# The decay of a chunk in a recurrence: applied to the state's sums instead of to `b` and `k`, with small operand steps on ScalarE

## The chip, the cores and the metric

The kernel runs on one core of one Trainium2 chip. The metric is the device time of one execution in microseconds. A run is one execution on the chip; the time of a kernel is the median of its runs.

## What is computed

The reference is two blocks of a network over 256 tokens of width 1024. The first block has two layers; each has a gated feed-forward part, a mixing part with a recurrence (RWKV-7, eight heads of 64) beside a block attention, a cross attention to a memory of 256 tokens, and a second feed-forward part. The second block (chunked mLSTM, differential attention, a mixture of experts) isn't touched. The change lies in the recurrence, which the reference states as a scan over tokens, cut here to its core:

```python
    kk = kk / jnp.maximum(jnp.sqrt(jnp.sum(kk * kk, axis=-1, keepdims=True)), 1e-12)
    b = kk * a

    def step(state, inp):
        r_t, w_t, k_t, v_t, kk_t, b_t = inp
        sa = jnp.einsum('bhij,bhj->bhi', state, -kk_t)
        state = (state * w_t[:, :, None, :] + sa[..., None] * b_t[:, :, None, :]
                 + v_t[..., None] * k_t[:, :, None, :])
        return state, jnp.einsum('bhij,bhj->bhi', state, r_t)
```

## The kernel before

All of it is one program in which each engine works through its own list. The weights of the projections are read from memory as `raw`, split by ScalarE into a high part `wh` and by VectorE into the rest `wl`, and multiplied on TensorE in three products (`wh` with `XH`, `wl` with `XH`, `wh` with `XL`); a unit of weights is 128x1024. These products, shown as `mm` or `acc` with `wh` or `wl`, are most of TensorE's time.

The recurrence is computed in chunks of 64 tokens. Each layer has two groups of four heads (group 0 and 1). For a group, `rwkv_early` builds the operands from the projections: decays as running products (`Pc`, and its inverse `rP`, both tiles `el`), `AR` (the rows of minus `kk` and of `r`, times the decay) and `BK` (`b` and `k`, divided by the decay), for two halves `t` of 128 tokens. `pe` holds `Pc` at the last token of each chunk. A chunk's first column of `AR` has no decay and is written by a step of its own over 128x2 elements. `rwkv_solve` inverts a small triangular matrix `W` for both halves on VectorE, in fourteen steps of a product and a sum (`t1k<-W`, `W<-W,t1k`); the result goes to memory and comes back as `c` (`c<-W`, four transfers on SyncE), and VectorE spreads it into `Y`.

`rwkv_chunk` then does one half: transposes of `Y`, three products that finish the inverse, the solution `ZW` of the chunk's own equations, the scores `gr`, the outputs `YL`, and for each chunk the sums `ST` of the state with, for the middle chunks, a matrix `M` that carries the state on. Before the change `BK` is first multiplied on GpSimd with the decay to the chunk's end (`bkh`, 128x256, two a half), transposed on TensorE and evicted as `bkt`; the sums `ST` are products with `bkt` that ScalarE copies out of PSUM, and `M` adds a diagonal of the decays (`dg`, a tile `t1k` from GpSimd). `rwkv_late` carries the state over the chunks 1 and 2, adds the state's part to `YL`, and normalises it. A reciprocal root of that normalisation is a power on GpSimd.

What stands where is set by a planner while the program is written out. All parts of the mixing stage (both groups, the projections, the block attention `moba` with its tiles `bi` and `sm`, the memory's keys) are generators. Each ends a piece with

```python
        yield 0.86, self.due(y, RH)
```

that is TensorE's cost of the next piece by an estimate, and the time at which what it needs will be there by the planner's own clock, which notes every instruction at L378. The weaver puts weight products in until the piece is due. So a due time that is dropped or moved changes what stands beside it on every engine. Since all instructions pass L378, rows of the profile carry that line, and the tiles' names tell them apart. The mixing stage of the first layer lies at about 200 to 420 us, that of the second at about 896 to 1116 us.

Of the kernel before, what the change touches and what calls it, by code (L numbers as in the profile page):

```python
# [13 lines left out]
AF = mybir.ActivationFunctionType  # L14
OP = mybir.AluOpType
# [4 lines left out]
P = 128  # L20
# [427 lines left out]
class Prog:  # L448
# [525 lines left out]
    def rwkv_early(self, l, g, lo, rT, kT, need):  # L974

        nc = self.nc
        tt, stt, ts = nc.vector.tensor_tensor, nc.vector.scalar_tensor_tensor, nc.vector.tensor_scalar
        mm, tr, act = nc.tensor.matmul, nc.tensor.transpose, nc.scalar.activation
# [8 lines left out]
        sq, d, rd = (self.k("el", 512) for _ in range(3))  # L987
# [4 lines left out]
        s = self.ps("tr")  # L992
# [22 lines left out]
        Pc, rP = self.k("el", 512), self.k("el", 512)  # L1015
# [10 lines left out]
        for b in range(2):  # L1026
            z = self.ps("tr")
# [11 lines left out]
        cut = lambda z, t: z.rearrange("p (b t c s) -> p t b c s", b=2, t=2, c=2)[:, t]  # L1039
        t3 = lambda z, t: z.rearrange("p (b t s) -> p t b s", b=2, t=2)[:, t]  # L1040
        pe = self.k("pe", 8)
        pev = pe.rearrange("p (t b c) -> p t b c", t=2, b=2)
        AR, BK = [], []
        for t in range(2):
            nc.vector.tensor_copy(pev[:, t], cut(Pc, t)[:, :, :, 63])
            ar = self.k("AR", 512).rearrange("p (b k c s) -> p b k c s", b=2, k=2, c=2)
            bk = self.k("BK", 512).rearrange("p (k b s) -> p k b s", k=2, b=2)
            for c in range(2):
                kc, pc = cut(kk, t)[:, :, c], cut(Pc, t)[:, :, c]
                stt(ar[:, :, 0, c, 1:], kc[:, :, 1:], -1.0, pc[:, :, :63], op0=OP.mult, op1=OP.mult)  # L1050
                ts(ar[:, :, 0, c, 0], kc[:, :, 0], -1.0, None, op0=OP.mult)
            arm = ar.rearrange("p b k c s -> p b k (c s)")
            stt(bk[:, 0], t3(bT, t), -0.5, t3(rP, t), op0=OP.mult, op1=OP.mult)
            stt(bk[:, 1], t3(kp, t), -1.0, t3(rP, t), op0=OP.mult, op1=OP.mult)
            tt(arm[:, :, 1], t3(rT, t), t3(Pc, t), op=OP.mult)
            AR.append(arm)
            BK.append(bk)
            yield 0, -0.8
# [4 lines left out]
    def rwkv_late(self, l, g, lo, E, rkp, vT, Y, need, C):  # L1063
# [20 lines left out]
        for cc in (1, 2):  # L1084
            sp = self.ps("acc")
            for b in range(2):
                mm(sp[:, b * 64:(b + 1) * 64], M[cc][:, bs(b)], ST[cc][:, b * 64:(b + 1) * 64], start=True, stop=True)
            tt(ST[cc + 1], sp[:, :128], ST[cc + 1], op=OP.add)
            yield 0.43, self.due(ST[cc + 1])


# [101 lines left out]
    def rwkv_chunk(self, g, t, E, vT, DT, YL, M, ST, W, small, solved):  # L1193
# [85 lines left out]
        tt(rv, rv, rp, op=OP.add)  # L1279
        yield 0.86, self.due(rv)  # L1280
        ZW = solve(1)

        bh = []
        for i in range(2):
            z = self.k("bkh", 256)
            nc.gpsimd.tensor_tensor(z.rearrange("p (h d) -> p h d", d=64), BK[t][:, i].rearrange("p b (c s) -> p (b c) s", c=2),
                                    pev[:, t].rearrange("p b c -> p (b c)")[:, :, None].to_broadcast([P, 4, 64]), op=OP.mult)
            bh.append(z)
        yield 0.86, 0

        gr = self.k("gr", 1024).rearrange("p (b k i s) -> p b k i s", b=2, k=2, i=2)
        for par, gp in enumerate(self.heads2(BK[t], AR[t], 1)):
            tt(gr[:, :, par], gp.rearrange("p (b i s) -> p b i s", b=2, i=2),
               self.cst("mr")[:, None, None, :].to_broadcast([P, 2, 2, P]), op=OP.mult)
        yield 0.95, self.due(*bh)
        tp = self.ps("tr")
        for b in range(2):
            tr(tp[:, bs(b)], bh[0][:, bs(b)], self.ident)
            tr(tp[:, bs(2 + b)], bh[1][:, bs(b)], self.ident)
        bkt = self.k("bkt", 512)  # L1300
        act(bkt, tp, AF.Copy)
        tb, tk = bkt[:, :256], bkt[:, 256:]
# [17 lines left out]
        for c_ in range(2):  # L1320
            cc = 2 * t + c_
            rows = slice(c_ * 64, c_ * 64 + 64)
            if cc in (1, 2):
                mp = self.ps("acc")
                for b in range(2):
                    mm(mp[:, bs(b)], ZW[rows, 1, 2 * b:2 * b + 2].rearrange("p h d -> p (h d)"), tb[rows, bs(b)],
                       start=True, stop=True)
                dg = self.k("t1k", 256)
                nc.gpsimd.tensor_tensor(q2(dg), both(self.ident, 2),
                                        pev[:, t, :, c_:c_ + 1].to_broadcast([P, 2, P]), op=OP.mult)  # L1330
                m = self.k("M", 256)
                tt(q2(m), q2(mp[:, :256]), both(self.cst("bd"), 2), op=OP.mult)
                tt(m, m, dg, op=OP.add)
                M[cc] = m
                yield 0.43, 0
            if cc < 3:
                qp = self.ps("acc")
                for h in range(4):
                    b, par = divmod(h, 2)
                    o = qp[par * 64:par * 64 + 64, b * 64:(b + 1) * 64]  # L1340
                    mm(o, tb[rows, hs(h)], ZW[rows, 0, h], start=True, stop=False)
                    mm(o, tk[rows, hs(h)], tv[rows, hs(h)], start=False, stop=True)
                ST[cc + 1] = self.k("ST", 128)
                act(ST[cc + 1], qp[:, :128], AF.Copy)
                yield 0.7, 0
        yield 0, 0.7

# [1033 lines left out]
    def beyond(self, state, out):  # L2381
# [13 lines left out]
        with self.tc.If(most > P):  # L2395
# [18 lines left out]

BUFS = dict(s16=4, s8=8, ss=2, rs=4, rh=6, s2=4, t1k=4, bi=1, sm=1, pt=1, nr=2,
            omu=1, lora=1, rkv=10, waup=1, gup=1, half=1, kaf=1, sg=1,
            el=5, pe=2, AR=3, BK=3, bkh=2,
            ak=1, tokv=2, bkt=2, RH=2, ZW=2, A=2, Y=2, X=2, T1=2, M=2, ST=3, gr=1, K=2,
            DT=2, YL=2, W=1, c16=2)

# [69 lines left out]
```

## Time and profile before

| | us |
|---|---|
| median of 3 runs | 1950.87 |
| lowest, highest | 1950.57, 1951.28 |
| the profiled run | 1949.61 |
| its span | 1947.6 |

The profile is of one execution. Its span is the time from the first instruction to the last; about 2 us lie around it. A wait is idle time of an engine just before an instruction, with the instruction that ended it (the releaser). The engines are PE (TensorE), DVE (VectorE), ACT (ScalarE), POOL (GpSimd) and SP (SyncE, which issues the transfers); matmul rows of TensorE overlap, so a product of 0.39 us starts about 0.23 us behind the last.

### The profile page before, as it was taken

How to read it: one execution, taken by the hardware profiler on the slowest of the kernel's cores; microseconds unless marked ns; L12 is line 12 of the kernel's file. 1: busy time of each engine (PE TensorE's matmuls, PEld its weight loads, DVE VectorE, ACT ScalarE, POOL GpSimd, SP SyncE). 2: the span in 40 equal slices, each digit the busy share in tenths (PEclk: the TensorE clock that was granted, in tenths of full speed). 3: DMA queues.
4: the chain of work that ended last, by engine and by line, in shares of the span. 5: the costliest groups of instructions: out<-in, count | busy, mean ns of one | idle time of the engine just before them, and what ended most of it. 6: DMA issues, size and time to landing. Idle time of an engine off the chain costs nothing.

```text
span 1947.6 us, 26262 instructions
## 1 busy us (share of the span) xinstructions
PE 1897.4 (97%) x9534; PEld 1532.9 (79%) x9534; DVE 1403.1 (72%) x2287; ACT 1059.3 (54%) x1606; POOL 73.3 (4%) x69
## 2 busy tenths in 40 slices
PE   8999999999999999999999999999999999999997
PEld 6888778888888878888787888888777786877775
DVE  6666787664666676666877655666687677999897
ACT  4444653655544444445536655444555546777674
POOL 0000011000000000000110000000001000000000
PEclk9999999999999999999999999999999999999999
DMA  8766432244566656665314253666564453999996
GB/s 280 249 223 226 128 126 68 86 155 159 172 211 222 216 205 215 220 213 173 134 41 127 97 189 117 222 221 215 183 202 139 150 182 139 337 340 360 332 337 223
DMA packets 114806, 381.41 MB, mean 196 GB/s; under 512 B 17080, under 2 KB 21864, under 8 KB 114544
## 3 DMA queue, kind: packets, MB, share of 16 engines
q1 hardware_dynamic: 114672, 379.68, 58.3%
q8 instruction: 77, 1.26, 0.3%
q14 instruction: 57, 0.47, 0.1%
HBM read 378.03 MB, written 3.17 MB: 196 GB/s over the span
## 4 chain that ended last, share of the span: by engine, by line
PE 76%; issue 11%; DVE 7%; ACT 2%; POOL 1%; DMA 1%; SPq 0%; DVEq 0%; POOLq 0%; ACTq 0%
PE mm L378 40%; PE acc L378 31%; PE tr L378 6%; DVE wl L378 3%; ACT wh L378 1%; POOL rs L378 1%; DVE el L378 1%; DVE s L378 1%; DMA raw<-in_w_dram 1%; DVE XL L378 0%; DVE t1k L378 0%; DVE AR L378 0%; DMA K<-in_mem_dram 0%; DMA x<-in_x_dram 0%; ACT s L378 0%
## 5 line engine op out<-in xcount | busy, mean ns | idle before, releaser
L378 DVE TENSOR_TENSOR wl<-raw,wh 128x1024 fp32r<-128x1024 f32 x648 | 785.2, 1223 | 320.2 <-ACT wh L378 317.2
L378 ACT ACTIVATE wh<-raw 128x1024 fp32r<-128x1024 f32 x648 | 676.3, 1057 | 522.6 <-PE mm L378 295.3
L378 PE MATMUL mm<-wh,XH 128*128 128x512 f32 (+1 forms) x1456 | 579.6, 400 | 3.0 <-ACT s L378 2.4
L378 PE MATMUL mm<-wl,XH 128*128 128x512 f32 (+1 forms) x1456 | 573.5, 394 | 2.6 <-DVE wl L378 2.1
L378 PE MATMUL mm<-wh,XL 128*128 128x512 f32 (+1 forms) x1456 | 571.3, 393 | 0.3
L378 PEld LDWEIGHTS mm<-wl,XH 128*128 128x128 f32 x1456 | 274.4, 188 | 65.7 <-DVE wl L378 10.7
L378 PEld LDWEIGHTS mm<-wh,XH 128*128 128x128 f32 x1456 | 274.7, 189 | 63.5 <-ACT s L378 3.8
L378 PEld LDWEIGHTS mm<-wh,XL 128*128 128x128 f32 x1456 | 274.2, 188 | 57.9 <-DVE XL L378 1.1
L378 PE MATMUL acc<-wh,X 128*128 128x512 f32 x352 | 143.0, 406 | 0.0
L378 PE MATMUL acc<-wh,T 128*128 128x512 f32 x352 | 139.1, 395 | 0.0
L378 PE MATMUL acc<-wl,X 128*128 128x512 f32 x352 | 139.1, 395 | 0.0
L378 PE MATMUL acc<-wl,XH 128*128 128x512 f32 x288 | 115.0, 399 | 2.9 <-DVE wl L378 2.7
L378 PE MATMUL acc<-wh,XH 128*128 128x512 f32 x288 | 114.5, 404 | 0.9 <-ACT XH L378 0.5
L378 PE MATMUL acc<-wh,XL 128*128 128x512 f32 x288 | 114.0, 396 | 0.0
L378 PE MATMUL acc<-wh,ah 128*128 128x512 f32 x256 | 85.7, 396 | 1.3 <-ACT ah L378 1.3
L378 DVE SCALAR_TENSOR_TENSOR el<-raw,vecs,el 128x512 f32<-128x512 f32 x84 | 63.1, 751 | 32.9 <-DMA raw<-in_w_dram 31.1
L378 PEld LDWEIGHTS acc<-wh,T 128*128 128x128 f32 x352 | 66.3, 188 | 15.9
L378 PEld LDWEIGHTS acc<-wl,X 128*128 128x128 f32 x352 | 66.4, 189 | 13.8
L378 PEld LDWEIGHTS acc<-wh,X 128*128 128x128 f32 x352 | 66.3, 188 | 13.4
L378 POOL TENSOR_TENSOR rs<-s,emh 128x2 f32<-128x2 f32 (+2 forms) x28 | 31.6, 1133 | 1147.3 <-DVE s L378 1144.7
L378 PEld LDWEIGHTS acc<-wl,XH 128*128 128x128 f32 x288 | 54.7, 190 | 18.3 <-DVE wl L378 7.5
L378 PEld LDWEIGHTS acc<-wh,XH 128*128 128x128 f32 x288 | 54.4, 190 | 12.5 <-ACT XH L378 1.2
(377 smaller groups left out, 2060.5 us busy)
## 6 DMA issues: line engine op xcount, KB each, us to landing
raw<-in_w_dram SPq DMA_DIRECT2D x696, 512.0 KB
ext<-ext SPq DMA_DIRECT2D x1, 2048.0 KB
K<-in_mem_dram SPq DMA_DIRECT2D x8, 256.0 KB
x<-in_x_dram SPq DMA_DIRECT2D x4, 256.0 KB
bi<-ext SPq DMA_DIRECT2D x4, 256.0 KB
sm<-ext SPq DMA_DIRECT2D x4, 256.0 KB
w<-gates SPq DMA_DIRECT2D x2, 512.0 KB
out_dram<-x SPq DMA_DIRECT2D x4, 256.0 KB
```

What stands on the lines that cost most here:

```text
L378: r = f(*args, **kw)
```

## The change

`BK` is no longer multiplied with the decay before it is transposed, so the eight `bkh` products of a layer and their tile are gone, and the transposes read `BK` itself, without waiting for a due time of `bkh`. The decay is applied to what is summed: the eviction of `ST` from PSUM is made in two halves of 64 columns with the decay of the chunk as a scale per partition, and in `rwkv_late` the addition of the carried state becomes two steps of 64 columns that scale the product and add. `M` then needs a plain identity in place of the diagonal of decays, so the four `t1k` products of GpSimd are gone as well. Two kinds of small steps move from VectorE to ScalarE: the copies `pe`, and the first column of `AR`.

```diff
--- before.py
+++ after.py
@@ -1042,13 +1042,13 @@
         pev = pe.rearrange("p (t b c) -> p t b c", t=2, b=2)
         AR, BK = [], []
         for t in range(2):
-            nc.vector.tensor_copy(pev[:, t], cut(Pc, t)[:, :, :, 63])
+            act(pev[:, t], cut(Pc, t)[:, :, :, 63], AF.Copy)
             ar = self.k("AR", 512).rearrange("p (b k c s) -> p b k c s", b=2, k=2, c=2)
             bk = self.k("BK", 512).rearrange("p (k b s) -> p k b s", k=2, b=2)
             for c in range(2):
                 kc, pc = cut(kk, t)[:, :, c], cut(Pc, t)[:, :, c]
                 stt(ar[:, :, 0, c, 1:], kc[:, :, 1:], -1.0, pc[:, :, :63], op0=OP.mult, op1=OP.mult)
-                ts(ar[:, :, 0, c, 0], kc[:, :, 0], -1.0, None, op0=OP.mult)
+                act(ar[:, :, 0, c, 0], kc[:, :, 0], AF.Copy, scale=-1.0)
             arm = ar.rearrange("p b k c s -> p b k (c s)")
             stt(bk[:, 0], t3(bT, t), -0.5, t3(rP, t), op0=OP.mult, op1=OP.mult)
             stt(bk[:, 1], t3(kp, t), -1.0, t3(rP, t), op0=OP.mult, op1=OP.mult)
@@ -1085,7 +1085,9 @@
             sp = self.ps("acc")
             for b in range(2):
                 mm(sp[:, b * 64:(b + 1) * 64], M[cc][:, bs(b)], ST[cc][:, b * 64:(b + 1) * 64], start=True, stop=True)
-            tt(ST[cc + 1], sp[:, :128], ST[cc + 1], op=OP.add)
+            for b in range(2):
+                sb = slice(b * 64, (b + 1) * 64)
+                stt(ST[cc + 1][:, sb], sp[:, sb], E.out[2][:, cc // 2, b, cc % 2:cc % 2 + 1], ST[cc + 1][:, sb], op0=OP.mult, op1=OP.add)
             yield 0.43, self.due(ST[cc + 1])
 
 
@@ -1279,24 +1281,18 @@
         tt(rv, rv, rp, op=OP.add)
         yield 0.86, self.due(rv)
         ZW = solve(1)
-
-        bh = []
-        for i in range(2):
-            z = self.k("bkh", 256)
-            nc.gpsimd.tensor_tensor(z.rearrange("p (h d) -> p h d", d=64), BK[t][:, i].rearrange("p b (c s) -> p (b c) s", c=2),
-                                    pev[:, t].rearrange("p b c -> p (b c)")[:, :, None].to_broadcast([P, 4, 64]), op=OP.mult)
-            bh.append(z)
         yield 0.86, 0
 
         gr = self.k("gr", 1024).rearrange("p (b k i s) -> p b k i s", b=2, k=2, i=2)
         for par, gp in enumerate(self.heads2(BK[t], AR[t], 1)):
             tt(gr[:, :, par], gp.rearrange("p (b i s) -> p b i s", b=2, i=2),
                self.cst("mr")[:, None, None, :].to_broadcast([P, 2, 2, P]), op=OP.mult)
-        yield 0.95, self.due(*bh)
+        yield 0.95, 0
+
         tp = self.ps("tr")
         for b in range(2):
-            tr(tp[:, bs(b)], bh[0][:, bs(b)], self.ident)
-            tr(tp[:, bs(2 + b)], bh[1][:, bs(b)], self.ident)
+            tr(tp[:, bs(b)], BK[t][:, 0, b], self.ident)
+            tr(tp[:, bs(2 + b)], BK[t][:, 1, b], self.ident)
         bkt = self.k("bkt", 512)
         act(bkt, tp, AF.Copy)
         tb, tk = bkt[:, :256], bkt[:, 256:]
@@ -1325,12 +1321,9 @@
                 for b in range(2):
                     mm(mp[:, bs(b)], ZW[rows, 1, 2 * b:2 * b + 2].rearrange("p h d -> p (h d)"), tb[rows, bs(b)],
                        start=True, stop=True)
-                dg = self.k("t1k", 256)
-                nc.gpsimd.tensor_tensor(q2(dg), both(self.ident, 2),
-                                        pev[:, t, :, c_:c_ + 1].to_broadcast([P, 2, P]), op=OP.mult)
                 m = self.k("M", 256)
                 tt(q2(m), q2(mp[:, :256]), both(self.cst("bd"), 2), op=OP.mult)
-                tt(m, m, dg, op=OP.add)
+                tt(q2(m), q2(m), both(self.ident, 2), op=OP.add)
                 M[cc] = m
                 yield 0.43, 0
             if cc < 3:
@@ -1341,7 +1334,8 @@
                     mm(o, tb[rows, hs(h)], ZW[rows, 0, h], start=True, stop=False)
                     mm(o, tk[rows, hs(h)], tv[rows, hs(h)], start=False, stop=True)
                 ST[cc + 1] = self.k("ST", 128)
-                act(ST[cc + 1], qp[:, :128], AF.Copy)
+                for b in range(2):
+                    act(ST[cc + 1][:, b * 64:(b + 1) * 64], qp[:, b * 64:(b + 1) * 64], AF.Copy, scale=pev[:, t, b, c_:c_ + 1])
                 yield 0.7, 0
         yield 0, 0.7
 
@@ -2414,7 +2408,7 @@
 
 BUFS = dict(s16=4, s8=8, ss=2, rs=4, rh=6, s2=4, t1k=4, bi=1, sm=1, pt=1, nr=2,
             omu=1, lora=1, rkv=10, waup=1, gup=1, half=1, kaf=1, sg=1,
-            el=5, pe=2, AR=3, BK=3, bkh=2,
+            el=5, pe=2, AR=3, BK=3,
             ak=1, tokv=2, bkt=2, RH=2, ZW=2, A=2, Y=2, X=2, T1=2, M=2, ST=3, gr=1, K=2,
             DT=2, YL=2, W=1, c16=2)
```

What each engine then has in its list: TensorE has the same products and transposes; GpSimd has 24 instructions less and VectorE 16 less; ScalarE has 8 `pe`, 16 `AR` and 12 more `ST`. The order differs in these places.

TensorE, first layer, at the start of group 1's chain: transposes of `Y` (`tr<-csts,Y`) and what stands around them. `K` are the memory's keys, `mm` with `wh` or `wl` the weight products. Before:

```order
L378 MATMUL mm_3293<-wh_3165,XL_3190 128x512
L378 MATMUL mm_3293<-wh_3165,XH_3189 128x512
L378 MATMUL mm_3293<-wl_3166,XH_3189 128x512
L378 MATMUL tr_3228<-csts,K_3224 128x128 x4
L378 MATMUL tr_3237<-csts,Y_2793 128x128 x4
L378 MATMUL mm_3293<-wh_3165,XL_3190 128x512
L378 MATMUL mm_3292<-wh_3296,XH_3189 128x512
L378 MATMUL mm_3293<-wh_3296,XH_3189 128x512
L378 MATMUL mm_3292<-wl_3297,XH_3189 128x512
L378 MATMUL tr_3244<-csts,Y_2876 128x128 x4
L378 MATMUL tr_3251<-csts,K_3226 128x128 x4
L378 MATMUL acc_3272<-X_3242,A_2794 128x128 x4
```

The transposes of `Y` stand among weight products and those of `K`. The same engine and place after:

```order
L378 MATMUL mm_3071<-wl_3141,XH_1754 128x512
L378 MATMUL mm_3071<-wh_3140,XL_1755 128x512
L378 MATMUL mm_3071<-wh_3140,XH_1754 128x512
L378 MATMUL mm_3071<-wl_3141,XH_1754 128x512
L378 MATMUL mm_3071<-wh_3140,XL_1755 128x512
L378 MATMUL tr_3169<-csts,Y_2815 128x128 x4
L378 MATMUL tr_3177<-csts,Y_2852 128x128 x4
L378 MATMUL acc_3190<-X_3174,A_2816 128x128 x4
L378 MATMUL acc_3198<-X_3182,A_2853 128x128 x4
L378 MATMUL acc_3206<-Y_2815,T_737_3195 128x128 x4
L378 MATMUL acc_3212<-Y_2852,T_739_3203 128x128 x4
L378 MATMUL acc_3218<-RH_2849,Y_2815 128x128 x4
```

Ahead of both stand weight products; the transposes of `K` are behind the chain now, and the products of the chain follow one another without weight products between.

ScalarE, first layer, group 1: the softmax of the block attention (`bi`, `sm`) with the copies of weights (`wh`) around it. Before:

```order
L378 ACTIVATE sm_3186,s_787_3360<-sm_3186,s_778_3312 128x128 x2
L378 ACTIVATE sm_3186,s_788_3363<-sm_3186,s_779_3315 128x256 x2
L378 ACTIVATE wh_3368<-raw_3294 128x1024
L378 ACTIVATE bi_3183<-bi_3183,s_792_3378 128x128 x2
L378 ACTIVATE bi_3183<-bi_3183,s_793_3382 128x256 x2
L378 ACTIVATE sm_3186<-sm_3186,s_794_3386 128x128 x2
L378 ACTIVATE sm_3186<-sm_3186,s_795_3390 128x256 x2
L378 ACTIVATE ZW_3399<-acc_3394 128x512
L378 ACTIVATE ZW_3406<-acc_3401 128x512
L378 ACTIVATE wh_3416<-raw_3336 128x1024
```

A weight copy stands between the exponentials and the normalisations, and the next behind two evictions. ScalarE at the normalisations after:

```order
L378 ACTIVATE bi_3348<-bi_3348,s_813_3491 128x128
L378 ACTIVATE XH_3362<-s_807_3469 128x4x128
L378 ACTIVATE s_810_3482,ss_3364<-K_3460 128x512
L378 ACTIVATE XH_3362<-s_809_3478 128x4x128
L378 ACTIVATE s_811_3484,ss_3364<-K_3462 128x512
L378 ACTIVATE bi_3348<-bi_3348,s_813_3491 128x128
L378 ACTIVATE bi_3348<-bi_3348,s_814_3495 128x256 x2
L378 ACTIVATE sm_3351<-sm_3351,s_815_3499 128x128 x2
L378 ACTIVATE sm_3351<-sm_3351,s_816_3503 128x256 x2
L378 ACTIVATE wh_3533<-raw_3156 128x1024
L378 ACTIVATE rkv_1981<-acc_3539,vecs 128x256
```

The squares of the keys (`s,ss<-K`) and the whole softmax now stand ahead of the next weight copy `wh_3533`.

VectorE, first layer, group 0, second half of the operands. Before:

```order
L378 SCALAR_TENSOR_TENSOR AR_2173<-el_2101,el_2091 128x2x63
L378 TENSOR_SCALAR AR_2173<-el_2101 128x2
L378 SCALAR_TENSOR_TENSOR AR_2173<-el_2101,el_2091 128x2x63
L378 TENSOR_SCALAR AR_2173<-el_2101 128x2
L378 SCALAR_TENSOR_TENSOR BK_2174<-el_2102,el_2092 128x256
L378 SCALAR_TENSOR_TENSOR BK_2174<-el_2103,el_2092 128x256
L378 TENSOR_TENSOR AR_2173<-rkv_1877,el_2091 128x2x128
L378 SCALAR_TENSOR_TENSOR rkv_1980<-tr_2182,omu_1786,sh_95 128x256
```

Each product of 63 columns is followed by a step of one column per head pair. The same engine and place after:

```order
L378 SCALAR_TENSOR_TENSOR AR_2173<-el_2101,el_2091 128x2x63 x2
L378 SCALAR_TENSOR_TENSOR BK_2174<-el_2102,el_2092 128x256
L378 SCALAR_TENSOR_TENSOR BK_2174<-el_2103,el_2092 128x256
L378 TENSOR_TENSOR AR_2173<-rkv_1877,el_2091 128x2x128
L378 SCALAR_TENSOR_TENSOR rkv_1980<-tr_2182,omu_1786,sh_95 128x256
L378 TENSOR_TENSOR Y_2221<-acc_2223,csts 128x2x128
```

The two steps of one column are gone from between the products; on ScalarE they stand behind an eviction `s<-mm`, and `pe` stands ahead of a weight copy.

## Rows read from the trace of the kernel before

**Rows 1.** the page, busy time by engine, and two groups of the costliest

```profile
PE 1897.4 (97%) x9534; PEld 1532.9 (79%) x9534; DVE 1403.1 (72%) x2287; ACT 1059.3 (54%) x1606; POOL 73.3 (4%) x69
...
L378 DVE TENSOR_TENSOR wl<-raw,wh 128x1024 fp32r<-128x1024 f32 x648 | 785.2, 1223 | 320.2 <-ACT wh L378 317.2
L378 ACT ACTIVATE wh<-raw 128x1024 fp32r<-128x1024 f32 x648 | 676.3, 1057 | 522.6 <-PE mm L378 295.3
```

**Rows 2.** TensorE's waits, 195 to 420 us: waited for: us, times, longest

```profile
PE tr L378 <- DVE el L378: 1.6, 1, 1.6
PE tr L378 <- DVE rkv L378: 1.5, 1, 1.5
...
PE tr L378 <- DVE YL L378: 1.0, 1, 1.0
PE tr L378 <- DMA K<-in_mem_dram: 0.7, 1, 0.7
PE acc L378 <- DVE BK L378: 0.7, 1, 0.7
...
PE mm L378 <- ACT XH L378: 0.2, 1, 0.2
```

**Rows 3.** timeline of TensorE: start, duration, instruction [idle before <-releaser]

```profile
327.47 0.44 PE L378 MATMUL tr<-csts,YL 128*128 128x128 f32 x2 [1.02 <-DVE YL L378]
...
339.62 1.04 PE L378 MATMUL tr<-csts,K 128*128 128x128 f32 x8
...
346.72 0.60 PE L378 MATMUL tr<-csts,Y 128*128 128x128 f32 x4
...
1042.56 0.63 PE L378 MATMUL tr<-csts,K 128*128 128x128 f32 x4 [0.67 <-DMA K<-in_mem_dram]
```

**Rows 4.** timeline of GpSimd, 225 to 345 us

```profile
241.59 3.91 POOL L378 TENSOR_TENSOR bkh<-BK,pe 128x256 f32<-128x256 f32 x2 [6.87 <-DVE BK L378]
...
277.51 1.27 POOL L378 TENSOR_TENSOR t1k<-csts,pe 128x256 f32<-128x256 f32 x2 [5.87 <-DMA c<-W]
```

**Rows 5.** timeline of VectorE, 234 to 250 us

```profile
235.63 0.16 DVE L378 COPY pe<-el 128x4 f32<-128x4 f32 x1
...
244.24 0.59 DVE L378 TENSOR_SCALAR AR<-el 128x2 f32<-128x2 f32 x1
```

**Rows 6.** tile AR: count, ns min/median/max, first and last start, form

```profile
L378 DVE TENSOR_SCALAR AR<-el x16: 156/160/590, 240.8 to 996.8; 128x2 f32<-128x2 f32 x16
...
L378 DVE TENSOR_TENSOR AR<-rkv,el x8: 409/418/840, 235.7 to 996.9; 128x256 f32<-128x256 f32 x8
```

**Rows 7.** tile ST, the same columns

```profile
L378 ACT ACTIVATE ST<-acc x12: 257/278/279, 301.7 to 1082.9; 128x128 f32<-128x128 f32 x12
```

**Rows 8.** timeline of ScalarE, 319 to 400 us

```profile
342.80 0.61 ACT L378 ACTIVATE s<-K 128x512 f32<-128x512 f32 x1
...
354.33 0.40 ACT L378 ACTIVATE bi<-bi,s 128x128 f32<-128x128 f32 x1 [1.45 <-DVE s L378]
...
358.80 1.48 ACT L378 ACTIVATE bi<-bi,s 128x128 f32<-128x128 f32 x4
...
394.87 0.47 ACT L378 ACTIVATE rkv<-acc,vecs 128x256 f32<-128x256 f32 x1 [0.38 <-PE acc L378]
```

**Rows 9.** timeline of VectorE, 319 to 365 us

```profile
327.56 0.22 DVE L378 TENSOR_TENSOR t1k<-W 32x72 f32<-32x72 f32 x1
...
338.44 1.63 DVE L378 TENSOR_TENSOR wl<-raw,wh 128x1024 fp32r<-128x1024 f32 x1
...
340.45 0.20 DVE L378 TENSOR_TENSOR W<-W,t1k 32x28 f32<-32x28 f32 x1
...
344.62 1.27 DVE L378 TENSOR_TENSOR Y<-c,csts 128x512 f32<-128x512 f32 x2
```

**Rows 10.** timeline of SyncE's queue, 323 to 345 us

```profile
340.68 2.68 SPq L378 DMA_DIRECT2D c<-W  x4
```

**Rows 11.** stretches of 10 us: busy by engine, PEclk granted, DMA share, GB/s

```profile
280.00:290.00 10.00, 8.36 (x50) 7.22 (x50) 9.05 (x20) 4.44 (x8) 0.00 (x0) 0.69 0.10 27
```

## The prediction

> **What bounds the kernel now.** First the busy times: TensorE works 97% of the span, no other engine over 72%, GpSimd 4% [rows 1]. So the change, which takes nothing from TensorE's own list, can only pay or cost where TensorE stands idle. Next, the list of its waits in the mixing stage of the first layer: some 8.5 us in eleven places, of which the list shows the larger ones [rows 2]. Two of them, 1.6 us behind `el` and 1.5 us behind `rkv`, and 0.7 us behind `BK`, end on VectorE steps that prepare the recurrence's operands; 1.0 us ends on `YL` (the recurrence's outputs of head group 0); 0.7 us on a transfer of `K` and 0.2 us on `XH`. The second layer shows the same pattern 696 us later: its wait for `K` is 0.67 us, at 1042.56 [rows 3], against the 0.7 us of the list. I therefore work out one layer and take it twice. Outside these two stages TensorE's order hardly moves, and I count nothing there.
>
> **What is taken from VectorE and GpSimd: gains.** Per layer GpSimd loses eight products with the decay (`bkh`) and four small diagonals (`t1k<-csts,pe`); VectorE loses four copies `pe` and eight `AR` columns, which go to ScalarE. What the GpSimd products cost is seen beside them: at 241.59 two `bkh` take 3.91 us [rows 4], and inside that time a VectorE step over two columns takes 0.59 us [rows 5], where such a step has a median of 0.16 us [rows 6]. VectorE's path to `rkv` holds two slow ones, each some 0.50 us from start to start, two fast ones and two `pe` copies, some 0.07 us each from start to start behind a row of 0.16 us [rows 5]: 2 x 0.50 + 4 x 0.07 = 1.3 us. All of it stands before waits of TensorE of 0.7 and 1.5 us [rows 2], so I count it whole: **-1.3 us** (-1.1 to -1.4). ScalarE takes the columns beside this: it has room, and each delays the step behind it by about 0.1 us, which the longer waits behind cover. In group 1 the product `AR<-rkv,el`, 840 ns at its slowest against a median of 418 ns [rows 6], is the one beside GpSimd's diagonals at 277.51 [rows 4]; it loses 0.4 us, the copies another 0.1 us, and a step of about 0.2 us comes in ahead of the scan. It lies before the wait for `el`, 1.6 us [rows 2]: **-0.4 us** (-0.3 to -0.5), allowing 0.1 us for `pe` on ScalarE ahead of an eviction.
>
> **The state's scaling.** An eviction of `ST` on ScalarE, 128x128 in 278 ns at the median [rows 7], becomes two of 128x64 with a scale read from memory. No row shows that form. The lower bound is one row's 0.28 us for both, the upper two rows of a scaled eviction of 128x256, 0.47 us each [rows 8]. I take 0.55 us for the pair, since half the columns lie nearer the lower row. Six such pairs a layer are +1.6 us on ScalarE. VectorE's addition of two states becomes two of half the width, four pairs a layer. Neither lies ahead of a wait of TensorE now; the matmuls on the state have evictions of other tiles around them. I carry the most of this, and three like places (a transpose waits for `bkt`, a product for `A`, `tokv` for `ak`), as small waits: **+0.65 us** (0.3 to 0.8). The Trainium skill (ScalarE: Activation LUTs, What ACT_TABLE_LOAD costs) gives 186 ns plus 0.833 ns a column for an activation, and some 93 ns more for a scale by pointer: 0.49 us for a row of 256 columns, near the 0.47 us of the trace, and 0.57 us for the pair if their overlap of 93 ns holds. The same page of the Trainium skill (Rules for kernel authors) sends plain multiplications to VectorE and speaks against this part; by it the sum would not move by 0.1 us, as long as ScalarE waits for TensorE there.
>
> **What the new order costs.** The planner weaves the recurrence with projections by its own costs, and dropping two due times has moved more than the edit shows. Three places count.
>
> (a) *The end of group 0.* One ScalarE copy of weights now stands ahead of the squares of `YL`, and one VectorE residual ahead of their sums, 1.06 and 1.22 us [rows 1]; before, they stood behind. The wait for `YL` is now 1.0 us [rows 2]. TensorE has 26 products ahead of it in place of 18 in two pieces, so part is covered: **+0.7 us** (0 to 1.4).
>
> (b) *The start of group 1.* Call T the second transpose of `YL`, 327.47 [rows 3]. Before, TensorE does 48 weight products, eight transposes of `s` up to 339.62 (some 12.15 us), then eight of `K`, the scores, 11 more products and four of `K`, and only at 346.72 the transposes of `Y` [rows 3]. That work covers the triangular solve on VectorE. In the new order 42 products and eight transposes stand there. A product is some 0.23 us, since 48 of them and about 1.2 us of transposes are the 12.15 us; less six it is 10.8 us, and the rest has gone behind the chain. The solve itself is not shortened: it runs from 327.56 to 340.65 [rows 9], 13.1 us; without the diagonals on GpSimd [rows 4] the residual beside one of them falls from 1.63 us [rows 9] to the usual 1.22 us [rows 1], less 0.4 us, and a small step of 0.2 us comes in: T + 12.9 us. Then its result goes through memory: four transfers, whose issues alone take 2.68 us [rows 10]. `Y` started 3.97 us after the solve's end [rows 9], but VectorE was busy until then, so that is the upper bound; the lower is the 2.2 us from the end of group 0's solve, 275.34, to 277.51, where GpSimd stopped waiting for these transfers [rows 4]. I take 3.0 us. The first half of `Y` (1.27 us for two [rows 9]) adds 0.65 us. `Y` is there at T + 16.6 us, TensorE at T + 10.8 us: a wait of 5.8 us (5.0 to 6.8), where 0.9 us stood behind `K` and `XH` [rows 2]: **+4.9 us** (4.1 to 5.9). What moved behind the wait can't win it back, since TensorE shows no wait from 346.72 to the end of the stage to fill.
>
> (c) *The chain of group 1 and the softmax.* The chain now runs without weight products in between, so two evictions in a row show: **+0.4 us** (0.2 to 0.6). The attention's softmax comes behind the scores, that is some 20 us later, and with the norms of `K` it stands on ScalarE ahead of the weight copy that TensorE needs 24 products later. Ahead of that copy ScalarE has the eight exponentials (354.33 to 358.80 less a weight copy between them, 3.4 us), four squares of `K` (0.61 us and a read of some 0.2 us each, 3.2 us), four `XH` of the same width (2.4 us) and the normalisations (twice four in 1.48 us) [rows 8], some 12.0 us; ahead of the first lie three VectorE steps of the width of a half of `Y`, 1.9 us [rows 9], between them some evictions of the chain, 0.7 us, and behind them the copy of 1.06 us [rows 1]: 15.7 us. TensorE has about 13 us until then (24 products at 0.23 us are 5.5 us, the rest the end of the chain as it stands in the trace): **+2.7 us** (1.5 to 3.5).
>
> On SyncE the next layer's gate weights and the bias now stand ahead of the weight transfers; two units are loaded ahead, and I cost it at nothing. If that cover is gone, it is up to 1 us.
>
> **Sum.** A layer: -1.3 - 0.4 + 0.65 + 0.7 + 4.9 + 0.4 + 2.7 = +7.65 us; both +15.3 us. The profiled run took 1949.61 us, so 1964.9 us; it was 1.26 us below the median, so 1966.2 us, say 1966. All bounds low: +4.2 us a layer, 1959; all high: +10.8 us, 1972.
>
> **Rivals.** *The new waits are hidden* (0.18). One place decides, TensorE at the transposes of `Y` in group 1. Were `Y` there by T + 10.8 us, because the solve runs further ahead of `YL` than I read, the 0.9 us of old waits would go too, and with no other loss the change leaves -1.3 - 0.4 - 0.9 = -2.6 us a layer: 1945.7. For it: VectorE loses work before the solve, and the 1.0 us behind `YL` shows that the outputs, not the solve, were last. Against: in the new order only the first of the solve's fourteen steps stands wholly ahead of `YL`. *Half of it* (0.14): the wait at `Y` is about 2.5 us, because transfers land at once and the solve's steps close up, and the softmax copy is nearly in time; +4.9 and +2.7 become about +1.6 and +0.8, and the layer is near +1.5 us: within 1947 to 1955. *The clock falls too* (0.14). After the waits at 277 to 283 us the granted clock is 0.69 in 280 to 290, the lower level of 1.2 GHz for a part of it [rows 11]; the longer wait before `Y` could do the same in each layer. A mean of 0.69 is 6.2 of the ten at 1.2 GHz and the rest at 2.4; TensorE was busy 84% of them, so 6.2 x 0.84 / 2 = 2.6 us is the price a layer: 1966.2 + 5.2 = 1971.4. Against: that row follows three waits and a transpose-bound stretch, and one wait between long busy stretches may do less. *The columns on ScalarE delay its evictions* and eat the first gain: 2.6 us more, 1968.8, inside the range.
>
> **How the numbers follow.** The forecast alone has 0.50 (1959 to 1972), the clock 0.14, the half case 0.14, the hidden waits 0.18, anything slower still 0.04. The range of 8 in 10 runs from 1946, which cuts off about half of the hidden case, to 1974. About 0.2% of the time, 3.9 us, is what a measurement can tell: faster 0.18, the same 0.14, slower 0.68.
>
> **What would show it.** In the trace after: no wait of TensorE behind `BK` and `rkv` worth over 1 us in each layer, a wait of 5 to 7 us at the transposes of `Y` about 20 us after the last `ST` of group 0, and one of 1.5 to 3.5 us behind `wh` some 45 us later. The forecast is wrong if the wait at `Y` is under 2 us, or if the moved work meets a wait that I have not seen.

## The result, and the profile after

The changed kernel takes 1967.65 us in the median of 5 runs (1965.17 to 1970.58); the kernel before, on the same chip, 1950.57 us (1948.84 to 1951.28). The ratio is 1.0088, with a 95% interval of 1.0076 to 1.0100: slower by 17.1 us, where the forecast was 1966 us. The profiled execution took 1970.58 us with a span of 1968.7 us, some 3 us more than the median.

The page after, busy time by engine, to set beside [rows 1]:

```profile
PE 1905.0 (97%) x9534; PEld 1537.2 (78%) x9534; DVE 1400.3 (71%) x2271; ACT 1066.8 (54%) x1642; POOL 49.6 (3%) x45
```

VectorE lost 2.8 us and GpSimd a third of its time, ScalarE gained 7.5 us. TensorE has the same 9534 instructions and is busy 7.6 us longer; the span grew by 21.1 us. So this is a story of waits of TensorE and of slower products. Its waits in the first layer's mixing stage, 195 to 440 us (us, times, longest):

```profile
PE tr L378 <- DVE Y L378: 5.6, 2, 5.0
PE mm L378 <- ACT wh L378: 1.9, 1, 1.9
PE tr L378 <- DVE el L378: 1.8, 1, 1.8
...
PE tr L378 <- DVE YL L378: 1.0, 2, 0.7
PE acc L378 <- ACT pt L378: 0.7, 1, 0.7
...
PE tr L378 <- DVE rkv L378: 0.5, 1, 0.5
...
PE acc L378 <- DVE BK L378: 0.3, 1, 0.3
PE acc L378 <- ACT X L378: 0.2, 1, 0.2
```

Beside [rows 2], `rkv` fell from 1.5 to 0.5 us and `BK` from 0.7 to 0.3 us, the waits for `K` and `XH` are gone, and two large ones are new: 5.6 us behind `Y` and 1.9 us behind `wh`, with 0.7 us behind `pt`. The list adds up to 14.6 us. That of before adds up to 8.2 us (not to the 8.5 us of the prediction). The second layer's reads the same within 0.4 us at each of these. The places in TensorE's timeline (start, duration, instruction [idle before <-releaser]):

```profile
283.28 3.30 PE L378 MATMUL acc<-X,A 128*128 128x128 f32 x16 [0.25 <-ACT X L378]
...
328.19 0.44 PE L378 MATMUL tr<-csts,YL 128*128 128x128 f32 x2 [0.30 <-DVE YL L378]
...
344.24 1.09 PE L378 MATMUL tr<-csts,Y 128*128 128x128 f32 x4 [4.96 <-DVE Y L378]
345.93 1.09 PE L378 MATMUL tr<-csts,Y 128*128 128x128 f32 x4 [0.60 <-DVE Y L378]
346.81 2.86 PE L378 MATMUL acc<-X,A 128*128 128x128 f32 x16
...
353.33 2.01 PE L378 MATMUL acc<-ZW,A 128*128 128x128 f32 x16
...
384.50 0.74 PE L378 MATMUL mm<-wh,XH 128*128 128x512 f32 x2 [1.89 <-ACT wh L378]
```

The prediction's T, the second transpose of `YL`, is 328.19 here. TensorE ran out of work at 344.24 - 4.96 = 339.28, that is T + 11.1 us (T + 10.8 us was forecast), and went on at T + 16.05 us (T + 16.6 us was forecast). What held it is on VectorE and in SyncE's queue, the rows that answer to [rows 9] and [rows 10]:

```profile
340.25 0.19 DVE L378 TENSOR_TENSOR W<-W,t1k 32x28 f32<-32x28 f32 x1
343.40 0.69 DVE L378 TENSOR_TENSOR Y<-c,csts 128x512 f32<-128x512 f32 x1 [1.19 <-DMA c<-W]
345.09 0.69 DVE L378 TENSOR_TENSOR Y<-c,csts 128x512 f32<-128x512 f32 x1 [0.99 <-DMA c<-W]
```

```profile
340.46 2.68 SPq L378 DMA_DIRECT2D c<-W  x4
```

The solve ends at 340.44. But for one residual of weights (`wl`, 1.23 us) VectorE then waits for the transfers, whose first half it can use 2.96 us after the solve's end and whose second half 4.65 us after it. No row of before showed that, because VectorE was still busy then. The four transfers copy straight from one on-chip tile (`W`) into another (`c16`): each is a single transfer, and the result doesn't pass through the chip's main memory, as "through memory" may suggest.

Last, the clock, stretches of 10 us (busy time by engine, PEclk granted, DMA share, GB/s):

```profile
280.00:290.00 10.00, 7.95 (x54) 7.57 (x54) 9.00 (x19) 4.93 (x10) 0.00 (x0) 0.83 0.26 80
340.00:350.00 10.00, 5.16 (x29) 4.82 (x30) 4.23 (x9) 3.04 (x6) 0.00 (x0) 0.66 0.39 112
...
380.00:390.00 10.00, 7.98 (x39) 5.52 (x38) 7.89 (x22) 7.60 (x18) 3.55 (x3) 0.83 0.38 118
```

After the wait behind `Y` the granted clock is 0.66 in the mean of 340 to 350 us, so TensorE runs at the lower level (1.2 GHz) for a part of it; the products `X,A` at 346.81 take 2.86 us. After the wait behind `wh` it is 0.83.

### The profile page after: what moved, and what is told of

It is laid out like the page before. It is cut to its first block, busy times and chain, and to the rows that moved or that the text cites. A ratio compares the mean times of both kernels' runs of the same rounds, so it can differ in the third digit from the quotient of the medians.

```text
span 1968.7 us, 26262 instructions
## 1 busy us (share of the span) xinstructions
PE 1905.0 (97%) x9534; PEld 1537.2 (78%) x9534; DVE 1400.3 (71%) x2271; ACT 1066.8 (54%) x1642; POOL 49.6 (3%) x45
## 4 chain that ended last, share of the span: by engine, by line
PE 76%; issue 11%; DVE 7%; ACT 3%; DMA 1%; POOL 1%; SPq 0%; DVEq 0%; ACTq 0%; POOLq 0%
PE mm L378 40%; PE acc L378 31%; PE tr L378 5%; DVE wl L378 3%; ACT wh L378 2%; DVE s L378 1%; DVE el L378 1%; DMA raw<-in_w_dram 1%; POOL rs L378 1%; DVE t1k L378 1%; DVE XL L378 0%; ACT s L378 0%; SPq L378 0%; DMA x<-in_x_dram 0%; DMA c<-W 0%
## 5 line engine op out<-in xcount | busy, mean ns | idle before, releaser
L378 PEld LDWEIGHTS mm<-wl,XH 128*128 128x128 f32 x1456 | 274.8, 189 | 68.1 <-DVE wl L378 12.9
L378 ACT ACTIVATE t1k<-mm,rh 128x256 f32<-128x256 f32 x80 | 38.0, 475 | 48.9 <-PE mm L378 48.9
```

What stands on the lines that cost most here:

```text
L378: r = f(*args, **kw)
```

## The experiments

Theory A is the forecast's: the changed work gains a few us, and the changed order, which the forecast puts down to dropped due times, costs about 20 us, above all in a wait behind `Y` of group 1 and in a softmax that stands ahead of a weight copy. Theory B: the work itself costs, above all the columns and scaled evictions on ScalarE. To tell them apart, the planner's choices were written down as a list of 2492 numbers, one for each piece that it weaves in (`t.n` is the number of a generator), and the weaver was made to follow such a list in place of its due times. Before's list gives before's order, after's list that of after; the two are permutations of each other and differ at 368 places, nearly all in the two mixing stages. All experiments were timed in 5 rounds beside the kernel before.

**The changed work in the order of before** (`e1_new_work_old_order`): the changed kernel, woven by before's list.

```diff
-        t = next((t for t in able if t.ready <= self.now + 1e-6), None)
-        if t is None:
-            t = min(able, key=lambda z: z.ready)
-            self.now = t.ready
+        self.turn = getattr(self, 'turn', -1) + 1
+        t = next(t for t in able if t.n == SEQ[self.turn])
+        self.now = max(self.now, t.ready)
```

> All instructions of the changed kernel, but the planner's choices are replaced by the list of those it made for the kernel before, so every engine's work stands where it stood before. Theory A (the loss is the new order: the wait for Y of group 1, the softmax ahead of a weight copy, and the clock behind them): the gains alone are left, 1.3 + 0.4 us a layer less about 0.3 us of small waits, so 1947.5 us (1944 to 1950), no wait behind Y over 0.7 us. Theory B (the new steps on ScalarE and the scaled additions cost the time, in whatever order): 1960 us or more.

Measured: 1946.53 us (1944.25 to 1949.72), ratio 0.9975 (0.9966 to 0.9984). **The work alone makes the kernel faster**, and this version beats both kernels. No wait behind `Y` or `wh` is in its list. Three of its rows from the start of group 0's chain and two from that of group 1:

```profile
278.13 0.63 PE L406 MATMUL mm<-wl,XH 128*128 128x512 f32 x1
...
281.66 1.09 PE L406 MATMUL tr<-csts,Y 128*128 128x128 f32 x8 [0.34 <-DVE el L406]
283.27 2.05 PE L406 MATMUL acc<-X,A 128*128 128x128 f32 x16 [0.52 <-ACT X L406]
...
343.16 0.63 PE L406 MATMUL tr<-csts,K 128*128 128x128 f32 x4 [0.71 <-DMA K<-in_mem_dram]
343.62 0.60 PE L406 MATMUL tr<-csts,Y 128*128 128x128 f32 x4
```

**The old work in the order of after** (`e2_old_work_new_order`): the kernel before with the same edit, woven by after's list.

> The instructions of the kernel before, in the list of choices that the planner made for the changed one. Theory A: the 5 us wait for Y, the 1.9 us behind wh and the clock behind them stay, and the gains are missing; 1970 us (1965 to 1976). Theory B: about 1951 us.

Measured: 1975.53 us (1974.79 to 1977.10), ratio 1.0126 (1.0110 to 1.0141), at the upper end of what was expected. The order alone costs 24 us on the old work and 1967.65 - 1946.53 = 21.1 us on the new. Its first layer's waits:

```profile
PE tr L405 <- DVE Y L405: 5.7, 2, 5.5
PE tr L405 <- DVE el L405: 2.6, 1, 2.6
PE mm L405 <- ACT wh L405: 1.9, 1, 1.9
PE tr L405 <- DVE rkv L405: 1.5, 1, 1.5
```

The waits behind `Y` and `wh` come with the order, and the 1.5 us behind `rkv` stay with the old work. That settles A against B: the order costs, and the work does not.

**Which part of the edit turns the order** can be told without the chip, because the list is made by the planner's own clock while the program is written out. If only the due time of `bkh` is dropped from the kernel before, the planner makes before's list, at all 2492 places. If only the small steps on ScalarE are put in (the copies `pe` alone, or the first columns of `AR` alone, or both), it makes after's list, at all 2492 places. The other way round, after's kernel with both kinds of steps back on VectorE has before's list. So A is right about the order, but not about where it comes from: the dropped due time moves nothing, and steps of about 0.2 us on another engine turn 368 choices. Just ahead of the first choice that differs, the planner's clock for ScalarE stands at 251.8 us in place of 246.6 us, since in its plan the steps wait there for VectorE's results and everything behind them on ScalarE waits with them.

**The two halves of the work, each alone in before's order.** `e3_steps_alone_old_order` has only the steps on ScalarE (`pe`, the columns of `AR`), `e4_sums_alone_old_order` only the decay on the sums.

```diff
-            nc.vector.tensor_copy(pev[:, t], cut(Pc, t)[:, :, :, 63])
+            act(pev[:, t], cut(Pc, t)[:, :, :, 63], AF.Copy)
...
-                ts(ar[:, :, 0, c, 0], kc[:, :, 0], -1.0, None, op0=OP.mult)
+                act(ar[:, :, 0, c, 0], kc[:, :, 0], AF.Copy, scale=-1.0)
```

> The kernel before, in its own order, with one part of the change: pe and the first columns of AR on ScalarE; the products bkh and the diagonals stay on GpSimd. Theory A: VectorE loses two columns of 0.59 us beside GpSimd and six steps of 0.07 us ahead of the waits for BK and rkv, unless GpSimd slows the next steps in their place: -0.5 to -1.2 us a layer, 1949 us (1948 to 1950.5). Theory B: slower than before by over 2 us.

> The kernel before, in its own order, with the other part: the decay on the sums, no work of it on GpSimd; pe and the columns of AR stay on VectorE. Theory A: the columns fall from 0.59 to 0.16 us (-0.9 us) and AR of group 1 from 0.84 to 0.42 us: -1.2 us a layer, 1948.2 us (1946.5 to 1950). Theory B: the two scaled halves of ST on ScalarE and the two additions on VectorE lie on the path, slower than before by over 2 us.

Measured: the steps alone 1949.49 us, ratio 0.9994 (0.9985 to 1.0003), no difference that can be told; the sums alone 1947.33 us, 0.9981 (0.9972 to 0.9990). The wait behind `rkv` says why: 1.38 us with the steps alone, 0.68 us with the sums alone, 0.55 us with both, from 1.51 us. (The wait behind `BK` goes the other way: 0.35 us with the steps alone, still 0.67 us with the sums alone.) With the steps alone VectorE reaches its own step to `rkv` 1.2 us sooner than before (245.26 in place of 246.44), as the prediction had it. But GpSimd has a product of its own on that path, and it stands behind the two `bkh`:

```profile
241.48 4.91 POOL L406 TENSOR_TENSOR bkh<-BK,pe 128x256 f32<-128x256 f32 x2 [6.73 <-ACT sh L406]
246.36 1.27 POOL L406 TENSOR_TENSOR rkv<-rkv,el 128x512 f32<-128x512 f32 x1
...
245.81 1.29 POOL L406 TENSOR_TENSOR rkv<-rkv,el 128x512 f32<-128x512 f32 x1 [11.10 <-DVE AR L406]
```

The first two rows are of the steps alone: GpSimd is busy with `bkh` until 246.36, a microsecond after VectorE's last `AR`, and beside GpSimd's next product (`rkv`) a residual `wl` on VectorE takes 2.10 us (1.41 us with the sums alone). The last row is of the sums alone, where the product waits only for VectorE's `AR`. So the larger part of the gain is the eight products that GpSimd no longer does, as far as such small ratios tell.

The sums alone are also the version that needs no list from elsewhere: the program that the planner itself makes for that half of the edit is the same, instruction for instruction. Without the small steps on ScalarE, the planner would have given 1947.33 us.

**The scores and the softmax put back ahead of the chain** (`e5_scores_early`): after's work and list, but with the attention's scores, four of the transposes of `K` and some ten weight products moved ahead of the transposes of `Y`, and three pieces with the softmax into the chain. Places of the list in the first layer (the second: 948 more):

```diff
 461
+466 487 488 489 490 491 492
 462 463 464 465
-466
+494
 467 468 469 470
+497
 471 472 473 474
+503
 475 476
...
```

> The changed kernel in its own order, but for one place a layer: the eleven pieces of the list that hold the scores of the block attention, the transposes of K, ten weight products and the softmax stand ahead of the transposes of Y and among the first pieces of the chain, as in the kernel before. Theory A: the wait at Y of 5.6 us a layer falls to about 1.2 us, and the clock that falls behind it stays up: -4.4 - 2.5 us a layer, 1954 us (1950 to 1961), if the products that are missing later do not open a wait behind wh again. Theory B (new steps): within 3 us of the changed kernel's 1967.65 us.

Measured: 1956.28 us (1954.68 to 1957.46), ratio 1.0027 (1.0018 to 1.0037): **11.4 of the 21.1 us go with this one place.** Its rows at `Y`, and its clock in the two stretches in which after's fell:

```profile
344.54 0.60 PE L405 MATMUL tr<-csts,Y 128*128 128x128 f32 x4
...
345.93 2.01 PE L405 MATMUL acc<-X,A 128*128 128x128 f32 x16
```

```profile
340.00:350.00 10.00, 8.58 (x60) 7.01 (x61) 9.56 (x23) 5.47 (x17) 0.00 (x0) 1.00 0.34 105
380.00:390.00 10.00, 10.00 (x65) 7.27 (x63) 7.93 (x20) 5.71 (x12) 2.01 (x2) 1.00 0.43 132
```

The transposes start when they did in after (344.54 against 344.24), but TensorE has worked until then, save for two waits of 0.66 us each, and it goes on at the full clock. From the transposes of `x` at the start of the stage to those at its end it is 220.72 us in place of 227.43 us.

**Only the weight copy ahead of the softmax** (`e6_copy_early`): after's list, with the next weight copy, the norms of `K` and some twenty products moved ahead of the softmax's exponentials.

```diff
 502
+504 505 506 509 510 511
 503
-504 505 506
 507 508
-509 510 511
 512
```

> The changed kernel in its own order, but for one place a layer: the pieces that make the copy wh behind the softmax, the norms of K and some 20 weight products stand ahead of the block attention's exponentials. Theory A: the wait behind wh of 1.9 us a layer goes, and the clock of 0.83 behind it stays up (about 1.4 us); the wait at Y is not touched: -1.9 - 1.4 us a layer, 1961 us (1958 to 1964). If the softmax then makes its own reader wait in its place: 1966 us. Theory B: no difference.

Measured: 1975.52 us (1972.64 to 1977.02), ratio 1.0124 (1.0109 to 1.0140). **A miss by 14 us**, and slower than after itself. The wait behind `wh` is gone, but two others stand where the softmax's results are read:

```profile
385.08 1.53 PE L405 MATMUL tr<-csts,bi 128*128 128x128 f32 x6 [0.92 <-ACT bi L405]
388.43 0.69 PE L405 MATMUL acc<-pt,rkv 128*64 128x128 f32 x2 [1.82 <-ACT pt L405]
...
390.00:400.00 10.00, 10.00 (x54) 7.77 (x54) 6.02 (x13) 4.19 (x9) 1.01 (x1) 0.81 0.44 144
```

With 0.8 us behind a second `pt` and 0.8 us behind `wl` in its list, it is 4.3 us in place of after's 2.8 us behind `wh`, `pt` and `wl`, which is some 3 us for both layers of the 7.9 us by which it is slower than after. The clock, back at 1.00 in after's 390 to 400 us, is 0.81, which has a part of the rest; not all of it could be placed. So what the copy waited for was not only in the wrong place on ScalarE: the softmax itself is late, since its scores come after the chain. The expectation had left out that the twenty products which it moved ahead would be missing when `bi` and `pt` were due.

**Unread products in the wait** (`e7_filler_at_Y`): after's list; five products of 128x512 that nobody reads are added to TensorE's work in each layer (ten rows in the trace, `tr<-start,csts`).

```diff
         yield solved
+        if g == 1 and t == 0:
+            self.busy(5, self.ident)
```

> The changed kernel in its own order, with five products of 128x512 that nobody reads on TensorE ahead of the transposes of Y in group 1, in each layer: they add work in the time that TensorE waits for Y, some 4.3 us of 5.0 us, and do not make Y come sooner. If the clock falls because TensorE stands idle there, it stays at 1.00 in that stretch and 2 to 2.9 us a layer are won: 1962.5 us (1961 to 1964). If the clock behind the wait costs nothing on the path, 1967 to 1968 us.

Measured: 1963.96 us (1962.67 to 1965.92), ratio 1.0068 (1.0055 to 1.0082), as expected: **3.7 us faster than after with more work**, if narrowly: its slowest run (1965.92) lies above the fastest of after (1965.17). The rows at the same place, and the clock:

```profile
338.39 3.59 PE L405 MATMUL tr<-start,csts 128*128 128x512 f32 x8
...
344.01 0.63 PE L405 MATMUL tr<-csts,Y 128*128 128x128 f32 x4 [0.63 <-DVE Y L405]
345.32 0.63 PE L405 MATMUL tr<-csts,Y 128*128 128x128 f32 x4 [0.68 <-DVE Y L405]
345.78 2.01 PE L405 MATMUL acc<-X,A 128*128 128x128 f32 x16
...
351.46 2.01 PE L405 MATMUL acc<-ZW,A 128*128 128x128 f32 x16
...
340.00:350.00 10.00, 8.69 (x55) 6.77 (x54) 5.32 (x10) 3.91 (x6) 0.00 (x0) 1.00 0.36 109
```

`Y` comes no earlier, but from its first transposes to `ZW,A` it is 7.45 us where after takes 9.09 us: 1.64 us less. Of that, 0.38 us is the second half of `Y`, which here comes 1.31 us behind the first in place of 1.69 us. From the second transposes of `Y` to `ZW,A` it is 6.14 us in place of 7.40 us, and in the second layer 6.14 us in place of 7.51 us: about 1.3 us a layer is the price of the clock behind the wait. The wait itself is still paid. The rest of the 3.7 us has no place that these rows show.

**Where the other 9.7 us of the order lie.** e5 is still 9.7 us above e1. Two more lists divide it: `e8_front_old` is e5 with the choices between the operands and the transposes of `Y` of group 1 sorted back into before's order, `e9_back_old` e5 with those behind the chain sorted back.

```diff
-for k in (298, 1246): SEQ[k:k + 163]
+for k in (298, 1246): sorted(SEQ[k:k + 163], key=place_in_before)
...
-for k in (477, 1425): SEQ[k:k + 107]
+for k in (477, 1425): sorted(SEQ[k:k + 107], key=place_in_before)
```

> The kernel of e5_scores_early, with the planner's choices between the end of the operands and the transposes of Y of group 1 sorted back into the order of the kernel before (both layers); what stands in that stretch and all that comes behind it stay as in e5. e5 takes 1956.28 us, the changed work in the old order 1946.53 us, so some 9.7 us, 4.9 us a layer, are open. Theory F (the rest lies in group 0: a wait of 1.8 us behind el and the low clock that then falls into the chain, X,A 3.3 to 3.6 us in place of 2.05 us): 1.5 + 1.4 us and up to 1 us of slower products behind, some 3 to 4 us a layer, so 1949 us (1947 to 1952), with the wait for el under 1 us. Theory R (the rest lies behind the transposes of Y: waits of 1.1 us for wl, 1.3 us for XH and XL, 0.7 us for pt): 1956 us (1954 to 1958).

> The other half of the same question: the kernel of e5_scores_early with the choices behind the chain of group 1 (to the end of the stage) sorted back into the order of the kernel before, all ahead of it as in e5. Theory F (the rest lies in group 0): 1955 us (1953 to 1957), with the wait for el of 1.8 us still there. Theory R (behind the transposes of Y): 1948 us (1946 to 1951), with the waits for wl, XH, XL and pt gone.

Measured: 1953.12 us (1950.95 to 1953.84), ratio 1.0007 (0.9998 to 1.0016), for e8; 1955.10 us (1951.42 to 1957.71), 1.0018 (1.0009 to 1.0027), for e9. The front gives 3.2 us, about half of what F expected and more than R did. The back gives 1.2 us, as F expected and far less than R did, and that can't be told from nothing, since the intervals of e9 and e5 overlap. So F is the nearer one, but the two gains don't make 9.7 us. In e9 e5's waits of 1.1 us for `wl` and 0.7 us for `pt` went, and a wait of 2.2 us behind another `pt` came, as it seems because the old back expects the softmax where the old front would have put it. Half an order doesn't carry half of its price. F's wait for `el` of 1.8 us stood in e8's first layer all the same:

```profile
281.33 1.09 PE L405 MATMUL tr<-csts,Y 128*128 128x128 f32 x8 [1.81 <-DVE el L405]
282.67 2.05 PE L405 MATMUL acc<-X,A 128*128 128x128 f32 x16 [0.25 <-ACT X L405]
```

That wait is no loss at all: see the last section. Beside e1, e8 has waits of 2.9 us a layer behind `wl`, `XL`, `XH` and `pt` that e1 doesn't have, and lacks 1.1 us behind `K` and `ST`, which makes 1.8 of the 3.3 us a layer by which it is slower. The rest of that, about 1.5 us a layer, stays open.

## Why the prediction was right

It named the right mechanism, the waits at `Y` and behind the softmax, and the right places. The number is closer than the terms: some that were counted did not come, and the clock, which was counted at nothing, came in their place. That part is luck. In us a layer:

| step of the prediction | forecast | measured | by |
|---|---|---|---|
| operands, ahead of `BK` and `rkv` | -1.3 | -1.30 | 0.67 to 0.35 and 1.51 to 0.53 |
| operands of group 1, ahead of `el` | -0.4 | -0.66 | 6.31 to 5.65, see below |
| new small waits | +0.65 | +0.25 | `X` alone |
| (a) `YL` | +0.7 | 0.0 | 1.02 to 0.72 + 0.30 |
| (b) `Y` of group 1 | +4.9 | +4.7 | 4.96 + 0.60 - 0.9 |
| (c) softmax ahead of `wh` | +2.7 | +2.6 | 1.89, and 0.73 behind `pt`, which had not been named |
| (c) evictions in group 1's chain | +0.4 | 0.0 | no wait there in e7, at the full clock |
| the clock behind (b) | a rival, +2.6 | +1.3 | e7 |
| the clock behind (c) | not named | +1.2 | after against e2 |

**The gains** came as worked out. The row of GpSimd's products at 241.59 [rows 4] is gone, and VectorE's products beside which it stood are back at their usual length; e3 and e4 divide the gain as the prediction did not, since it followed VectorE's path to `rkv` alone and left out GpSimd's own product on it. The wait behind `el`, in contrast, did not fall (1.6 to 1.8 us). What fell is the time from the transposes of `t1k` to those of `Y` in group 0. Two rows of before, two of after:

```profile
276.93 0.74 PE L378 MATMUL tr<-csts,t1k 128*128 128x128 f32 x4 [0.67 <-ACT t1k L378]
283.24 1.97 PE L378 MATMUL tr<-csts,Y 128*128 128x128 f32 x8 [1.64 <-DVE el L378]
...
276.29 0.74 PE L378 MATMUL tr<-csts,t1k 128*128 128x128 f32 x4 [0.67 <-ACT t1k L378]
281.94 1.09 PE L378 MATMUL tr<-csts,Y 128*128 128x128 f32 x8 [1.80 <-DVE el L378]
```

That is 283.24 - 276.93 = 6.31 us before and 281.94 - 276.29 = 5.65 us after. TensorE's products ahead of it ran faster too, so more of a shorter stretch is waiting. With the sums alone (e4) the time is 5.18 us, with the steps alone (e3) 6.02 us: in this place the steps on ScalarE give back 0.47 us of what the sums win.

**The scaled sums** on ScalarE are off TensorE's path, as forecast. The pair takes 0.52 us where 0.55 us was taken:

```profile
371.01 0.52 ACT L378 ACTIVATE ST<-acc,pe 128x64 f32<-128x64 f32 x2 [1.78 <-PE acc L378]
```

The 0.57 us that the Trainium skill (ScalarE: Activation LUTs, What ACT_TABLE_LOAD costs) gives for the pair is 10% above that.

**The wait behind `Y`** was the step on which the sign rested, and both of its sides were read well: TensorE's 42 products and eight transposes (T + 10.8 us forecast, T + 11.1 us measured), and the solve with its transfers (T + 16.6 us forecast, T + 16.05 us measured). The solve itself ended at T + 12.25 us (T + 12.9 us forecast). The 3.0 us taken for the transfers were 2.96 us for the first half. What was missed is that the second half can be used 1.7 us later, a second wait of 0.60 us in the first layer and 0.20 us in the second. **The softmax ahead of the copy** was right in place and in sum; e6 shows that the reason was narrower than the truth, since moving the copy doesn't save it.

**The rival of the clock** is true in part, beside the forecast: its price behind `Y` was 1.3 us a layer where 2.6 us was named. A second fall, behind `wh`, had not been named. e2 has after's list and the same wait of 1.89 us there, but its clock stayed at 1.00 in 380 to 390 us, where after's was 0.83. One row of after, then three of e2:

```profile
392.56 1.52 PE L378 MATMUL acc<-pt,rkv 128*64 128x128 f32 x12
...
387.38 0.73 PE L405 MATMUL mm<-wh,XH 128*128 128x512 f32 x2 [1.89 <-ACT wh L405]
394.22 1.52 PE L405 MATMUL acc<-pt,rkv 128*64 128x128 f32 x12
380.00:390.00 10.00, 7.98 (x57) 5.16 (x56) 8.72 (x26) 9.26 (x24) 1.43 (x2) 1.00 0.21 46
```

From the end of the wait to these products it is 392.56 - 384.50 = 8.06 us in after and 394.22 - 387.38 = 6.84 us in e2: 1.2 us, and as much in the second layer.

**The sum.** The terms that the forecast counted measure 5.6 us a layer in place of 7.65 us. The clock adds 1.3 us behind `Y`, 1.2 us behind `wh`, and 0.55 us in group 0's chain (6.27 to 6.82 us from the first transposes of `Y` to the end of `Y,T`, in the two profiled executions): 8.6 us a layer, 17.2 us in all, where the medians show 17.1 us. But the profiled execution of after is 2.9 us above its median, and its two stages are 9.7 and 9.4 us longer than those of before, so about 0.9 us a layer of these rows has no place.

**What was wrong in kind.** The order did not come from the dropped due times but from the small steps on ScalarE, which the prediction counted only as work. The two rivals that hide the waits failed because the solve did not run further ahead, as the prediction's count of its steps had it. That ScalarE's evictions are delayed by the columns shows in no total time (e3: no difference).

## What to carry to other kernels

Where a planner sets the order, a few steps of 0.2 us that change engines can cost more by the order that they turn than the work gains: here the work gained 4 to 5 us and the order cost 21 us. So keep the old order beside the new work as a version of its own (e1: faster than both kernels), before the work is judged. And ask the planner which part of the edit moves its list, which needs no chip: here it was the part with the smaller gain, and without it (e4) the planner keeps the old order by itself. Ahead of a chain that begins with transfers, count what TensorE has to do until they can be used, and remember that what is moved behind the wait comes late for its own readers too.

## What was not expected of the hardware

**A wait after slow products may cost nothing, and a wait after fast ones may cost twice.** In after, e1 and e5 to e9, which have the new work whole, the time from the transposes of `t1k` to those of `Y` in group 0 is 5.65 or 5.66 us, whatever wait the profile shows ahead of the latter: 0.34 us in e1's first layer, 0.82 us in e8's second, 1.80 us in after. Where the wait is short, the products ahead of it stood 0.43 us apart in place of 0.23 us (e1, 278.13: 0.63 us each), that is, the low clock fell on work that had to wait anyway. Where they ran at the full clock, the wait was longer, and the low clock came after it: `X,A` 3.30 us in after in place of 2.05 us in e1. But not always: behind the same wait of 1.8 us `X,A` took 2.05 us in the first layers of e8, e9 and e6, and in the second of e7. e6 and e7 have after's order up to that place, so the order alone doesn't decide it. What does, these runs don't show.

**Products that nobody reads made the kernel 3.7 us faster** (e7, against after). The granted clock held through the wait, 1.00 in place of 0.66 in 340 to 350 us, and about 1.3 us a layer of the gain is that.

**Four small transfers from tile to tile can be used in two steps**, since SyncE issues them one after another, in 2.68 us. In after's first layer the first half of `c` could be used 2.96 us after the last step of the solve and the second 4.65 us after it (4.27 us in its second layer; 4.31 and 4.27 us in e7).
